# Deferring x0's scale and shift through DRAM, and moving GpSimd steps to VectorE, in a two-block transformer kernel

## The chip, the core and the metric

The kernel runs on one core of one Trainium2 chip. The metric is the device time of one execution in microseconds (us): the median of several runs, smaller is better. The core's compute engines are TensorE (PE in the profile; PEld is its weight load), VectorE (DVE), ScalarE (ACT) and GpSimd (POOL). SyncE (SP) issues the transfers between the chip's memory (DRAM) and the on-chip buffer. Each engine works through its own instructions in program order and waits for others by semaphores.

## The reference, cut to what matters

The sequence has T = 1024 rows of width D = 1024, in fp32. Two transformer blocks stand behind each other; the change touches the first up to the end of its mixer:

```python
x = layer_norm(x, ln0_g, ln0_b)                       # "x0"
mod = silu(c) @ w_ada + b_ada
sh_a, sc_a, gt_a, sh_f, sc_f, gt_f = split(mod, 6)    # 1024 columns each
h = x * (1.0 + sc_a) + sh_a
y = hybrid_mixer(h, w_in, ...)                        # gated delta rule (4 heads) and gated linear attention
x = layer_norm(ALPHA * x + (1.0 + gt_a) * y, ln1_g, ln1_b)
...                                                   # conv FFN, third norm, second block
```

In the mixer, `h @ w_in` gives q, k, v (through a short causal convolution and silu), gates and the inputs of the linear attention (GLA). The delta rule needs its decay gates (`log_a`, `beta`) before any head can start.

## The kernel before

Every large product runs as three fp32r products on PE (`mm3`, line 415): an operand is split into a high part (a cast on ACT, line 430) and a low part (a subtraction, line 433, on DVE unless a caller names POOL). PE transposes through line 419.

The order of the instructions is not written by hand. Parts of the work are Python generators, "streams", which a small planner (`Order`) interleaves: a stream yields a time or a condition, the planner's clock advances with each matmul that is emitted, and the stream due first goes on. When a stream is written with other yields, or emits other instructions, the rows of each engine interleave in another way. On-chip memory is handed out in pages (`Arena`): 128x1024 "full" or 128x512 "half"; the names pa, pg, y, wh, wl, wf in the rows are pages, opl and oph the low and high part of a left operand, b a PSUM bank.

What the change touches, in the order of time:

- `startup` normalizes x, makes the columns `sh_a`, `sc_a` from w_ada with multiply-adds on DVE (lines 765 and 767), and makes the first operand block by block: transposes on PE, then two ACT copies (lines 790, 791) and the subtraction for the low part (line 792, POOL). `w_take("A0")` splits the first weights.
- `x0_out` scales and shifts the normalized rows: for each of eight pages one DVE multiply (line 857) and one POOL add (line 858), then a store to `x0_d`. These rows are read back much later, behind the mixer.
- `delta_gates` (lines 1172 to 1212) makes the gates with some fifteen tiny DVE operations on 128x32 tiles (`dg_...`); the last one writes `dg_la` (line 1182), which PE needs for cumulative sums (`b<-dg_la,triu`), and with them the first head can start. The convolutions of q, k, v stand on the same engine: multiply-adds from PSUM (line 574), finished by line 1021.
- `mod_rest` makes the other four parts of `mod`, in eight chunks of 512 columns: eight loads of w_ada (256 KB each, two ahead) per chunk, each scaled on ACT (line 881) and added up on POOL (line 883; the first is copied, line 885).
- In the delta rule each unit of half a head has three POOL products of 128x512 (lines 1475, 1487, 1488), GLA one per head (line 1291). The gated output (`gate_op`) splits into high and low parts, with every second low part on POOL.

Of the kernel before, what the change touches and what calls it, by code (L numbers as in the profile page):

```python
# [169 lines left out]
def p3(ap, b=P):  # L170
    return ap.rearrange("p (a b) -> p a b", b=b)
# [139 lines left out]
class Kern:  # L311
# [398 lines left out]
    def startup(self):  # L710
# [38 lines left out]
        for h in range(2):  # L749
            for _ in self.ln_rows([p.ap for p in x[4 * h:4 * h + 4]]):  # L750
                pass
        wa = self.w_take("A0")
        hs, hb, tb = self.sm(), self.sm(), self.sm()
# [18 lines left out]
        def feed(k, acc):  # L772

            pm = self.ps()
            for c in (1, 0):
                for i in range(2):
                    self.mm(pm[:, c:c + 1], acc[:, i, c], self.ones[:, 0:1], i == 0, i == 1)

            c1 = slice(k, k + 1)
            V.scalar_tensor_tensor(hs[:, c1], pm[:, 1:2], b1[:, c1], self.ln0_g[:, c1], op0=OP.add, op1=OP.mult)  # L780
            V.scalar_tensor_tensor(tb[:, c1], pm[:, 1:2], b1[:, c1], self.ln0_b[:, c1], op0=OP.add, op1=OP.mult)
            V.scalar_tensor_tensor(hb[:, c1], pm[:, 0:1], self.b_ada[:, c1], tb[:, c1], op0=OP.add, op1=OP.add)
            self.psg(pm)
            for hf in range(2):
                h, l = self.op[hf]
                ps = self.ps()
                for t in range(4):
                    self.tr(ps[:, t * P:(t + 1) * P], x[4 * hf + t].ap[:, k * P:(k + 1) * P])
                f = fl[hf].ap
                S.activation(h[:, k], ps, AF.Identity, scale=hs[:, c1], bias=hb[:, c1])  # L790
                S.activation(f, ps, AF.Identity, scale=hs[:, c1], bias=hb[:, c1])
                G.tensor_tensor(out=l[:, k], in0=f, in1=h[:, k].bitcast(F32), op=OP.subtract)  # L792
                self.psg(ps)
# [9 lines left out]
        for j, ks in enumerate(blocks):  # L803
            acc = products(j)
            ada_load(1)
            for i, k in enumerate(ks):
                feed(k, acc[:, :, :, i * P:(i + 1) * P])
                if k:
                    use(k - 1)
# [14 lines left out]
    def start_rest(self):  # L824
        G = self.nc.gpsimd
        self.fb()
        G.tensor_scalar(self.hgain[:, 0:1], self.dnng, 0.5, None, op0=OP.mult)
        G.tensor_scalar(self.hgain[:, 1:2], self.glng, 0.5, None, op0=OP.mult)
        yield from self.x0_out(self.x)
        yield from self.mod_rest(self.cond)  # L830

# [7 lines left out]
    def x0_out(self, x):  # L839

        nc, I, A = self.nc, self.I, self.A
        self.x0_d = self.dram.tile([T, D], F32, name="x0_d")
        gr, br = self.gb
        for r, n in ((gr, "ln0_g"), (br, "ln0_b")):
            self.row_of(r.ap, I[n])
        yield 2.31
        nc.vector.tensor_scalar(br.ap, br.ap, ALPHA, None, op0=OP.mult)

        def out(t):
            nc.sync.dma_start(self.x0_d[t * P:(t + 1) * P, :], x[t].ap)  # L850
            A.give(x[t])
            self.x0_out_done.add(t)
            return
            yield
        for t in range(8):
            p = x[t].ap
            nc.vector.scalar_tensor_tensor(p, p, ALPHA, gr.ap, op0=OP.mult, op1=OP.mult)
            nc.gpsimd.tensor_tensor(p, p, br.ap, OP.add)
            self.o.spawn(out(t), 8)
            yield 3.92  # L860
        A.give(gr, br)

    def mod_rest(self, cond):
# [5 lines left out]
        for c in range(4, 12):  # L869
# [6 lines left out]
            for k in range(KT):  # L876
# [3 lines left out]
                a = wh[k % 3].ap  # L880
                nc.scalar.activation(a, a, AF.Copy, scale=cond[:, k:k + 1])
                if k:
                    nc.gpsimd.tensor_tensor(acc, acc, a, OP.add)  # L883
                else:
                    nc.gpsimd.tensor_copy(acc, a)
            A.give(*wh[1:])
# [377 lines left out]
    def gla_unit(self, p, hf, gls, q, k, gvp, att, St):  # L1264
# [25 lines left out]
        V.scalar_tensor_tensor(qd, q[:, hs], 0.125, t, op0=OP.mult, op1=OP.mult)  # L1290
        G.tensor_tensor(kn, k[:, hs], kdt, OP.mult)
        V.tensor_tensor(ke, ke, k[:, hs], OP.mult)
# [132 lines left out]
    def delta(self, h, kq, vp):  # L1425
# [10 lines left out]
        for hf in range(2):  # L1436
# [37 lines left out]
            V.scalar_tensor_tensor(Mn, Mn, 0.0, mb(self.mL), op0=OP.max, op1=OP.add)  # L1474
            G.tensor_tensor(qd, qd, p3(q_[:, c0 * P:(c0 + 4) * P]), OP.mult)
            S.activation(u["at"].ap, u["at"].ap, AF.Exp)
# [9 lines left out]
            V.tensor_scalar(nbr2, br2, -1.0, None, op0=OP.mult)  # L1486
            G.tensor_tensor(xk, kd, bc(xkc), OP.mult)
            G.tensor_tensor(kd, kd, bc(self.ekd[:, hc]), OP.mult)
            V.tensor_tensor(Mn, Mn, bc(nbr2), OP.mult)
# [206 lines left out]
    def gate_op(self, hf, k, z, done):  # L1696
# [7 lines left out]
        self.psg(ps)  # L1704
        self.split(z, h[:, k], l[:, k], lo_eng=G if k % 2 else V)
        self.A.give(*done)
# [96 lines left out]
    def x_ops(self, ready, free, evs, kept=None):  # L1803
# [5 lines left out]
        add, sub = OP.add, OP.subtract  # L1809
        yield ready  # L1810
        t3, t4, pages = [], [], []
        for j in range(4):
# [265 lines left out]
    def ffn(self, sc):  # L2078
# [70 lines left out]
        yield self.h2[0]  # L2149
        self.o.spawn(self.x_ops(self.h2[1], two, tev, self.xf))  # L2150
        self.o.spawn(self.res_rows(tev[1]))
# [1046 lines left out]
```

## Time and profile before

| | before |
|---|---|
| median of three runs | 2696.44 us (2691.53 to 2700.05) |
| profiled execution, its time | 2694.74 us |
| its span (first to last instruction) | 2693.0 us |
| mean granted TensorE clock | 0.989 |
| busy: PE, DVE, ACT, POOL | 95%, 73%, 49%, 15% |

The profiled execution is the one whose rows are read below; its own time stands 1.7 us over its span and 1.7 us under the median of the runs. A busy share is an average over the whole span. POOL has most of its work in the first quarter; DVE's share differs from stretch to stretch.

### The profile page before, as it was taken

Reading aid. Unit: us, or ns where it says so; the run is one execution under the profiler, and the core shown is the slowest. Engines: PE = TensorE matmul, PEld = TensorE weight load, DVE = VectorE, ACT = ScalarE, POOL = GpSimd, SP = SyncE. Lnnn points to the kernel's source line nnn. Section 1 sums busy time; section 2 is a strip of 40 time slices with the busy share of each in tenths; the row PEclk is TensorE's granted clock in tenths of the full one; section 3 lists DMA queues with packets and bytes.
Section 4 is the critical chain, followed back from the end, with each engine's and each line's share of the span. In section 5 each row is a group of like instructions: output and inputs, shape, how many; then the busy total and the mean of one; then the engine's idle time right before and its main releaser. Section 6 shows DMA issues by size and latency. Waiting matters only on the chain.

```text
span 2693.0 us, 35990 instructions
## 1 busy us (share of the span) xinstructions
PE 2569.3 (95%) x13053; PEld 2094.2 (78%) x13053; DVE 1954.4 (73%) x3264; ACT 1317.6 (49%) x2261; POOL 413.4 (15%) x472
## 2 busy tenths in 40 slices
PE   6889999999999999999989999999999999999998
PEld 4677888789877777788867666679878888888886
DVE  7875565457798897798976876775546866788774
ACT  4434544344544444464357867774444433344443
POOL 4633333332000000000140232310000000000002
PEclk9999999999999999999999999999999999999999
DMA  7423323565433433365311312166204345484541
GB/s 229 158 58 97 86 75 93 160 217 175 132 117 129 156 118 103 140 216 155 110 55 43 82 50 62 49 201 195 77 32 141 137 126 167 178 295 131 171 125 63
DMA packets 293218, 343.95 MB, mean 128 GB/s; under 512 B 32401, under 2 KB 217513, under 8 KB 293041
## 3 DMA queue, kind: packets, MB, share of 16 engines
q1 hardware_dynamic: 292656, 341.51, 39.9%
q8 instruction: 103, 1.69, 0.3%
q14 instruction: 74, 0.61, 0.1%
q10 hardware_dynamic: 385, 0.15, 0.0%
HBM read 244.12 MB, written 93.28 MB: 125 GB/s over the span
## 4 chain that ended last, share of the span: by engine, by line
PE 70%; DVE 13%; ACT 5%; POOL 4%; DMA 3%; issue 3%; SPq 0%; POOLq 0%; DVEq 0%; ACTq 0%
PE b L415 67%; PE b L419 3%; DVE wl L433 2%; POOL smalls L597 1%; DVE pg L2118 1%; DVE y L2118 1%; ACT wh L430 0%; POOL y L883 0%; DVE y L574 0%; DMA pa<-in_w_ada_dram 0%; DVE wf L2118 0%; DMA wf<-in_w_o_dram 0%; DMA pg<-in_w_ada_dram 0%; POOL rsv L596 0%; DVE y L2057 0%
## 5 line engine op out<-in xcount | busy, mean ns | idle before, releaser
L415 PE MATMUL b<-oph,wl 128*128 128x512 f32 (+1 forms) x1552 | 623.2, 403 | 12.2 <-ACT oph L670 8.6
L415 PE MATMUL b<-opl,wh 128*128 128x512 f32 (+1 forms) x1552 | 612.9, 395 | 0.6 <-POOL opl L792 0.6
L415 PE MATMUL b<-oph,wh 128*128 128x512 f32 (+1 forms) x1552 | 609.8, 393 | 0.0
L415 PEld LDWEIGHTS b<-oph,wl 128*128 128x128 f32 x1552 | 293.6, 189 | 77.4 <-ACT oph L670 8.8
L415 PEld LDWEIGHTS b<-opl,wh 128*128 128x128 f32 x1552 | 293.4, 189 | 62.3 <-issue 3.1
L415 PEld LDWEIGHTS b<-oph,wh 128*128 128x128 f32 x1552 | 293.0, 189 | 62.8 <-issue 1.5
L415 PE MATMUL b<-opl,oph 128*128 128x512 f32 x672 | 261.4, 389 | 0.0
L415 PE MATMUL b<-oph 128*128 128x512 f32 x672 | 261.4, 389 | 0.0
L415 PE MATMUL b<-oph,opl 128*128 128x512 f32 x672 | 261.3, 389 | 0.0
L430 ACT CAST oph<-pg 128x512 fp32r<-128x512 f32 (+1 forms) x202 | 125.4, 629 | 233.2 <-PE b L415 203.8
L415 PE MATMUL b<-wh,opl 128*128 128x256 f32 (+1 forms) x608 | 198.0, 326 | 0.9 <-DVE opl L433 0.7
L415 PE MATMUL b<-wl,oph 128*128 128x256 f32 (+1 forms) x608 | 193.5, 318 | 0.0
L415 PE MATMUL b<-wh,oph 128*128 128x256 f32 (+1 forms) x608 | 193.3, 318 | 0.0
L433 DVE TENSOR_TENSOR opl<-pg,oph 128x512 fp32r<-128x512 f32 (+1 forms) x210 | 144.1, 695 | 64.0 <-ACT oph L430 62.4
L433 DVE TENSOR_TENSOR wl<-wf,wh 128x1024 fp32r<-128x1024 f32 (+2 forms) x98 | 132.8, 1355 | 63.6 <-ACT wh L430 63.4
L430 ACT CAST wh<-y 128x512 fp32r<-128x512 f32 x164 | 101.9, 622 | 127.5 <-PE b L415 108.9
L430 ACT CAST wh<-wf 128x1024 fp32r<-128x1024 f32 (+2 forms) x98 | 112.4, 1147 | 79.9 <-PE b L415 46.0
L433 DVE TENSOR_TENSOR wl<-y,wh 128x512 fp32r<-128x512 f32 x164 | 112.7, 691 | 49.3 <-ACT wh L430 48.9
L415 PEld LDWEIGHTS b<-oph 128*128 128x128 f32 x672 | 126.1, 188 | 26.4
L415 PEld LDWEIGHTS b<-oph,opl 128*128 128x128 f32 x672 | 126.1, 188 | 26.4 <-ACT y L1993 0.2
L415 PEld LDWEIGHTS b<-opl,oph 128*128 128x128 f32 x672 | 126.1, 188 | 26.0
L415 PEld LDWEIGHTS b<-wh,opl 128*128 128x128 f32 x608 | 116.4, 192 | 11.1 <-issue 2.2
(1117 smaller groups left out, 5145.4 us busy)
## 6 DMA issues: line engine op xcount, KB each, us to landing
pg<-s_d SPq DMA_DIRECT2D x168, 256.0 KB
wf<-in_w_in_dram SPq DMA_DIRECT2D x48, 512.0 KB
y<-in_ffn_w_up_dram SPq DMA_DIRECT2D x31, 512.0 KB
s_d<-pg SPq DMA_DIRECT2D x31, 512.0 KB
s_d<-y SPq DMA_DIRECT2D x20, 512.0 KB
y<-in_w_mlp_in_dram SPq DMA_DIRECT2D x20, 512.0 KB
pa<-in_w_ada_dram SPq DMA_DIRECT2D x39, 256.0 KB
dn<-in_w_mlp_out_dram SPq DMA_DIRECT2D x18, 512.0 KB
```

The costliest lines, as they stand in the source:

```text
L415: self.nc.tensor.matmul(o, a, b, start=start, stop=stop, **kw)
L419: self.nc.tensor.transpose(o, a, self.ident if ident is None else ident)
L430: nc.scalar.copy(hi, src)
L433: (lo_eng or nc.vector).tensor_tensor(out=lo, in0=src, in1=hi.bitcast(F32), op=OP.subtract)
L597: nc.gpsimd.tensor_tensor(out, v[:, :n], self.mhalf[:, :n], OP.pow)
L2118: V.scalar_tensor_tensor(t[:, d:], x[:, :T - d], tap(2 - d, m), t[:, d:], op0=OP.mult, op1=OP.add)
```

## The change

The scale and shift of x0 no longer stand in `x0_out`: the normalized pages are stored to a scratch tensor in DRAM (`xh_d`) and given back at once. A new stream, `x0_rows`, starts 110 us of planner time later and does the work in 16 pieces of 128x512: load from `xh_d`, DVE multiply, DVE add, store to `x0_d`. In `mod_rest`, the ACT scaling and POOL addition of each piece become one DVE multiply-add. The low parts of the first operand, three products per delta rule unit, one product per GLA head, and the remaining low parts of `gate_op` move from POOL to DVE. `w_take("A0")` stands after the first block of the operand. Another edit, in `x_ops`, only makes an argument lazy.

```diff
164.09 1.11 PE L419 MATMUL b<-ident,pa 128*128 128x128 f32 x4 [6.10 <-DVE pa L1021] startup
-        wa = self.w_take("A0")
+        wa = []
...
-                G.tensor_tensor(out=l[:, k], in0=f, in1=h[:, k].bitcast(F32), op=OP.subtract)
+                V.tensor_tensor(out=l[:, k], in0=f, in1=h[:, k].bitcast(F32), op=OP.subtract)
...
                 feed(k, acc[:, :, :, i * P:(i + 1) * P])
+                if not k:
+                    wa += self.w_take("A0")
...
         yield from self.x0_out(self.x)
+        yield 25
         yield from self.mod_rest(self.cond)
164.09 1.11 PE L419 MATMUL b<-ident,pa 128*128 128x128 f32 x4 [6.10 <-DVE pa L1021] x0_out
-            nc.vector.scalar_tensor_tensor(p, p, ALPHA, gr.ap, op0=OP.mult, op1=OP.mult)
-            nc.gpsimd.tensor_tensor(p, p, br.ap, OP.add)
-            self.o.spawn(out(t), 8)
-            yield 3.92
-        A.give(gr, br)
+            self.nc.sync.dma_start(self.xh_d[t * P:(t + 1) * P, :], x[t].ap)
+            self.A.give(x[t])
+        self.A.give(*self.gb)
+        self.o.spawn(self.x0_rows())
...
+    def x0_rows(self):
+        nc, A, V = self.nc, self.A, self.nc.vector
+        yield 110
+        for c in range(2):
+            cs = slice(c * 512, (c + 1) * 512)
+            yield self.need(0, 3)
+            gb = A.half(), A.half()
+            for r, n in zip(gb, ("ln0_g", "ln0_b")):
+                self.row_of(r.ap, self.I[n][cs])
+            yield 5
+            for r in gb:
+                V.tensor_scalar(r.ap, r.ap, ALPHA, None, op0=OP.mult)
+            for t in range(8):
+                yield self.need(0, 1)
+                pg = A.half()
+                rows = slice(t * P, (t + 1) * P)
+                nc.sync.dma_start(pg.ap, self.xh_d[rows, cs])
+                yield 6
+                V.tensor_tensor(pg.ap, pg.ap, gb[0].ap, OP.mult)
+                V.tensor_tensor(pg.ap, pg.ap, gb[1].ap, OP.add)
+                nc.sync.dma_start(self.x0_d[rows, cs], pg.ap)
+                A.give(pg)
+                yield 8
+                if c:
+                    self.x0_out_done.add(t)
+            A.give(*gb)
164.09 1.11 PE L419 MATMUL b<-ident,pa 128*128 128x128 f32 x4 [6.10 <-DVE pa L1021] mod_rest
-                nc.scalar.activation(a, a, AF.Copy, scale=cond[:, k:k + 1])
                 if k:
-                    nc.gpsimd.tensor_tensor(acc, acc, a, OP.add)
+                    V.scalar_tensor_tensor(acc, a, cond[:, k:k + 1], acc, op0=OP.mult, op1=OP.add)
                 else:
-                    nc.gpsimd.tensor_copy(acc, a)
+                    V.tensor_scalar(acc, a, cond[:, 0:1], None, op0=OP.mult)
164.09 1.11 PE L419 MATMUL b<-ident,pa 128*128 128x128 f32 x4 [6.10 <-DVE pa L1021] GLA, delta rule, gate_op
-        G.tensor_tensor(kn, k[:, hs], kdt, OP.mult)
+        V.tensor_tensor(kn, k[:, hs], kdt, OP.mult)
...
-            G.tensor_tensor(qd, qd, p3(q_[:, c0 * P:(c0 + 4) * P]), OP.mult)
+            V.tensor_tensor(qd, qd, p3(q_[:, c0 * P:(c0 + 4) * P]), OP.mult)
...
-            G.tensor_tensor(xk, kd, bc(xkc), OP.mult)
-            G.tensor_tensor(kd, kd, bc(self.ekd[:, hc]), OP.mult)
+            V.tensor_tensor(xk, kd, bc(xkc), OP.mult)
+            V.tensor_tensor(kd, kd, bc(self.ekd[:, hc]), OP.mult)
...
-        self.split(z, h[:, k], l[:, k], lo_eng=G if k % 2 else V)
+        self.split(z, h[:, k], l[:, k])
```

How instructions move shows at three places. First VectorE, where the decay gates are made, before:

```order
L1021 SCALAR_TENSOR_TENSOR pa_103<-pa_101,pa_103 128x1024
...
L433 TENSOR_TENSOR wl_74<-wf,wh_73 128x1024
L1175 TENSOR_TENSOR dg_x<-dg_x,rb 128x32
...
L857 SCALAR_TENSOR_TENSOR y<-y,pa_98 128x1024
L1202 TENSOR_SCALAR dg_u<-dg_e 128x32
L857 SCALAR_TENSOR_TENSOR y<-y,pa_98 128x1024
L574 SCALAR_TENSOR_TENSOR pg<-b_77,hcv,pg 128x511
L1204 TENSOR_SCALAR dg_u<-dg_u 128x32
L857 SCALAR_TENSOR_TENSOR y<-y,pa_98 128x1024
...
L1212 SCALAR_TENSOR_TENSOR dg_x<-dg_x,dg_l 128x32
L1452 TENSOR_REDUCE smalls<-pa_106 128x4
L1182 SCALAR_TENSOR_TENSOR dg_la<-dg_x,dg_ea 128x32
```

And the same place in the changed program, whose lines stand 17 or 18 further down (its lines 900 and 902 are the multiply-add and the first product of `mod_rest`):

```order
L433 TENSOR_TENSOR wl_74<-wf,wh_73 128x1024
L1038 SCALAR_TENSOR_TENSOR pa_103<-pa_101,pa_103 128x1024
...
L574 SCALAR_TENSOR_TENSOR pg<-b_77,hcv,pg 128x511
L1227 TENSOR_TENSOR dg_l<-dg_l,dg_e 128x32
L902 TENSOR_SCALAR wh_630<-wh_630,cond 128x512
L574 SCALAR_TENSOR_TENSOR pg<-b_77,hcv,pg 128x510
L1228 TENSOR_TENSOR dg_l<-dg_l,dg_u 128x32
L900 SCALAR_TENSOR_TENSOR wh_630<-wl_631,cond,wh_630 128x512
L574 SCALAR_TENSOR_TENSOR pg<-b_77,hcv,pg 128x509
L1229 SCALAR_TENSOR_TENSOR dg_x<-dg_x,dg_l 128x32
L900 SCALAR_TENSOR_TENSOR wh_630<-wl_631,cond,wh_630 128x512
L1199 SCALAR_TENSOR_TENSOR dg_la<-dg_x,dg_ea 128x32
```

The 128x1024 multiplies of `x0_out` are gone from between the gate operations; three operations of `mod_rest` on freshly loaded pieces of w_ada stand there instead, and the subtraction for the weights has moved ahead of the second convolution's end (line 1021, now 1038). Second, PE at the gates: the block of matmuls into bank b_75 (q, k, v and z projections), before:

```order
L419 MATMUL b_80<-ident,pa_104 128x128 x4
L415 MATMUL b_75<-oph_66,wl_74 128x512
...
L415 MATMUL b_75<-opl_67,wh_73 128x512
L415 MATMUL b_75<-oph_66,wh_73 128x512
L415 MATMUL b_81<-dg_la,triu 128x32
L415 MATMUL b_81<-dg_la,ones 128x32
```

And in the changed program:

```order
L419 MATMUL b_80<-ident,pa_104 128x128 x4
L415 MATMUL b_75<-oph_66,wl_74 128x512
L415 MATMUL b_81<-dg_la,triu 128x32
L415 MATMUL b_81<-dg_la,ones 128x32
L415 MATMUL b_75<-opl_67,wh_73 128x512
L415 MATMUL b_75<-oph_66,wh_73 128x512
```

Before, nine matmuls of that block (the first two and last two rows stand around the mark) come ahead of the gate products, now one does: PE asks for `dg_la` eight matmuls earlier. Third, the queue of SyncE ahead of the gates in the changed program (wf is the next block of w_in, wh_630 and wl_631 the first pieces of w_ada for `mod_rest`):

```order
L846 DMA xh_d<-y 128x1024 x3
L463 DMA wf<-in_w_in_dram 128x8x128
L846 DMA xh_d<-y 128x1024 x3
L463 DMA wf<-in_w_in_dram 128x8x128
L846 DMA xh_d<-pg 128x1024 x2
L1434 DMA t_d_704<-y 128x344 x3
...
L463 DMA wf<-in_w_in_dram 128x8x128
L891 DMA wh_630<-in_w_ada_dram 128x512
L891 DMA wl_631<-in_w_ada_dram 128x512 x2
```

The loads for `mod_rest` stand right behind a load of wf, and a load of wf waits until DVE has read the wf before it (line 433). Before, the eight stores of x0 stood among and behind these loads, each waiting for POOL's add; now they stand ahead and wait for no engine's arithmetic on x0.

## Rows read from the trace of the kernel before

**Rows 1.** The page: busy per engine; share by engine of the chain; one group.

```profile
PE 2569.3 (95%) x13053; PEld 2094.2 (78%) x13053; DVE 1954.4 (73%) x3264; ACT 1317.6 (49%) x2261; POOL 413.4 (15%) x472
...
PE 70%; DVE 13%; ACT 5%; POOL 4%; DMA 3%; issue 3%; SPq 0%; POOLq 0%; DVEq 0%; ACTq 0%
...
L433 DVE TENSOR_TENSOR opl<-pg,oph 128x512 fp32r<-128x512 f32 (+1 forms) x210 | 144.1, 695 | 64.0 <-ACT oph L430 62.4
```

**Rows 2.** Waits of PE, 70 to 690 us: total us, times, longest us.

```profile
PE b L415 <- DVE dg_la L1182: 9.2, 1, 9.2
PE b L419 <- DVE pa L1021: 6.1, 1, 6.1
PE b L415 <- DVE y L1552: 3.9, 2, 2.7
...
PE b L419 <- DVE pg L1703: 0.2, 1, 0.2
```

**Rows 3.** Timeline of PE at the two large waits: start us, us, [idle before].

```profile
108.02 0.64 PE L415 MATMUL b<-dg_la,triu 128*128 128x32 f32 x2 [9.23 <-DVE dg_la L1182]
...
109.46 0.63 PE L415 MATMUL b<-opl,wh 128*128 128x512 f32 x1
109.89 0.63 PE L415 MATMUL b<-oph,wh 128*128 128x512 f32 x1
...
112.84 0.40 PE L415 MATMUL b<-oph,wh 128*128 128x512 f32 x1
113.08 0.40 PE L415 MATMUL b<-oph,wl 128*128 128x512 f32 x1
...
164.09 1.11 PE L419 MATMUL b<-ident,pa 128*128 128x128 f32 x4 [6.10 <-DVE pa L1021]
```

**Rows 4.** Timeline of DVE around the gates, 84 to 114 us.

```profile
84.95 2.68 DVE L1021 SCALAR_TENSOR_TENSOR pa<-pa,pa 128x1024 f32<-128x1024 f32 x1
...
88.88 1.21 DVE L433 TENSOR_TENSOR wl<-wf,wh 128x1024 fp32r<-128x1024 f32 x1
90.01 2.40 DVE L1175 TENSOR_TENSOR dg_x<-dg_x,rb 128x32 f32<-128x32 f32 x1
...
106.23 1.73 DVE L1182 SCALAR_TENSOR_TENSOR dg_la<-dg_x,dg_ea 128x32 f32<-128x32 f32 x1
...
110.70 0.18 DVE L1191 TENSOR_TENSOR dg_u<-b,Gc 128x32 f32<-128x32 f32 x1
...
113.96 0.74 DVE L574 SCALAR_TENSOR_TENSOR pg<-b,hcv,pg 128x509 f32<-128x509 f32 x1
```

**Rows 5.** Timeline of POOL in the same stretch.

```profile
88.92 3.44 POOL L858 TENSOR_TENSOR y<-y,pa 128x1024 f32<-128x1024 f32 x1
```

**Rows 6.** Groups of instructions, 0 to 70 us, DVE, then POOL.

```profile
L767 DVE SCALAR_TENSOR_TENSOR pa<-pa,cond,pa 128x512 f32<-128x512 f32 x6 | 8.1, 1421 | 0.0
L767 DVE SCALAR_TENSOR_TENSOR y<-pa,cond,y 128x512 f32<-128x512 f32 x6 | 6.1, 1083 | 0.0
...
L792 POOL TENSOR_TENSOR opl<-pa,oph 128x512 fp32r<-128x512 f32 x15 | 23.3, 1573 | 15.9 <-ACT pa L791 15.8
```

**Rows 7.** Busy time by stretch: length, then each engine's.

```profile
70.00:110.00 40.00, 30.77 (x139) 21.11 (x138) 38.25 (x54) 15.19 (x25) 21.62 (x11) 0.91 0.51 172
...
300.00:690.00 390.00, 377.23 (x2431) 329.29 (x2430) 231.24 (x409) 169.67 (x286) 119.22 (x139) 0.99 0.44 139
```

**Rows 8.** ACT's scaling in mod_rest (L881): idle before it until, us, times.

```profile
  DMA pg<-in_w_ada_dram: 26.4, 13
  DMA pa<-in_w_ada_dram: 18.9, 14
...
  DMA y<-in_w_ada_dram: 8.7, 3
```

**Rows 9.** One piece of w_ada: SP issues it.

```profile
213.86 0.35 SPq L873 DMA_DIRECT2D pa<-in_w_ada_dram  x1
```

**Rows 10.** The same piece: ACT has it.

```profile
216.95 0.72 ACT L881 ACTIVATE pa<-pa,cond 128x512 f32<-128x512 f32 x1 [1.35 <-DMA pa<-in_w_ada_dram]
```

More of the change, by code (lines that the diff above doesn't have):

```diff
@@ L839, in x0_out @@
     def x0_out(self, x):
-        nc, I, A = self.nc, self.I, self.A
         self.x0_d = self.dram.tile([T, D], F32, name="x0_d")
[L843 to L854, printed above, removed]
-        for t in range(8):
-            p = x[t].ap
-            nc.vector.scalar_tensor_tensor(p, p, ALPHA, gr.ap, op0=OP.mult, op1=OP.mult)
-            nc.gpsimd.tensor_tensor(p, p, br.ap, OP.add)
-            self.o.spawn(out(t), 8)
-            yield 3.92
-        A.give(gr, br)
+        for t in range(8):
+            self.nc.sync.dma_start(self.xh_d[t * P:(t + 1) * P, :], x[t].ap)
+            self.A.give(x[t])
+        self.A.give(*self.gb)
+        self.o.spawn(self.x0_rows())
+        return
+        yield
+    def x0_rows(self):
[24 more added lines that the diff above has]
+            A.give(*gb)
     def mod_rest(self, cond):
@@ L1810, in x_ops @@
         yield ready
+        kept = kept and kept()
         t3, t4, pages = [], [], []
@@ L2149, in ffn @@
         yield self.h2[0]
-        self.o.spawn(self.x_ops(self.h2[1], two, tev, self.xf))
+        self.o.spawn(self.x_ops(self.h2[1], two, tev, lambda: self.xf))
         self.o.spawn(self.res_rows(tev[1]))
```

## The prediction

> **What bounds the kernel now.** I read the page first: PE is busy 95% of the span, and the chain that ended last runs through PE for 70% of its length, through DVE for 13% and through POOL for 4% [rows 1]. So the time is PE's matmuls plus the gaps between them, and since the matmuls are not changed, an edit is worth what it does to PE's gaps. The second view is therefore the waits of PE over the stretch that the change touches. There the reader is to see two large ones and many small: 9.2 us for `dg_la`, 6.1 us for a convolution that line 1021 finishes (that of v for head 1), and 19 further groups from 3.9 down to 0.2 us, 20.7 us together [rows 2]. Nearly all are waits for DVE, whose work is late, not for POOL, whose work the change mostly moves.
>
> The third view is PE's timeline at the largest wait. PE stands from 98.79 to 108.02 for the gates, and afterwards its 512-column matmuls start 0.43 us apart (109.46, 109.89) before they are back at 0.24 (112.84, 113.08) [rows 3]. The first is the pitch of the lower clock level (1.2 GHz), the second that of the upper (2.4 GHz). From 108.02 to 112.84 PE worked at half speed, so the idle time costs another 2.4 us.
>
> The fourth view is DVE in the same stretch: it has hardly any idle time (38.25 of 40 us busy from 70 to 110 [rows 7]) and is late because of what stands between the gate operations. Six of the eight multiplies of x0 lie ahead of `dg_la`, each at least the 1.2 us of the like operation at 88.88; and tiny operations take far longer than they need. The addition of 128x32 at 90.01 took 2.40 us, the multiply-add that writes `dg_la` 1.73, where a like operation at 110.70 took 0.18 [rows 4]. At 90.01 POOL's add of x0, begun at 88.92, was running until 92.36 [rows 5], and the DVE addition ends 0.05 us behind it.
>
> **The change, part by part.** The total that moves to DVE: 16 low parts, 32 half-page operations for x0 instead of 8 multiplies of 1.2 us and one page of scaling, 64 multiply-adds, 28 products, 8 low parts of `gate_op`. By 0.695 us for a two-input operation of 128x512 [rows 1] and 0.74 for a multiply-add [rows 4] this is 11 + (22 + 2 - 10) + 47 + 19 + 6 = 97 us more on an engine that is busy 1954 us. Against it stand the collisions with POOL that go. What counts is where each lies.
>
> *The gates (term 1).* Ahead of `dg_la`, six multiplies (7 us) and the collisions (2.40 against 0.18, 1.73 against 0.18 and the like) go; one product and two multiply-adds of `mod_rest` come, at most 2.2 us. From the second convolution's end (begun at 84.95, 1.2 us without a collision) `dg_la` needs 2.5 us of tiny operations (some 14 at 0.18), three multiply-adds from PSUM (2.2) and those 2.2: ready at 93 if nothing else is waited for. But the first piece of w_ada is now in the way: its load stands behind a load of wf, which waits for the DVE subtraction that I read at 88.88, 1.21 us long [rows 4]; so it is issued at 87.5 (if that subtraction moves ahead of the second convolution, as the order shows) to 90.5. A piece landed 3.1 us after its issue (213.86 to 216.95) [rows 9, 10]. The product then starts at 91 to 94, and 2.5 to 3 us of DVE work stand between it and `dg_la`: ready at 94 to 97. PE asks for it eight matmuls of 0.24 us earlier than before, at 98.79 - 1.9 = 96.9. The gap is 0 to 1.5 us if these rows hold, and up to 4 if the stores of x0, 4 MB now issued at once, hold the pieces back. I take 1.0: 9.2 becomes 1.0, **-8.2 us**; with no gap of that length the slow clock behind it goes too, **-2.4** (bounds 0 and -2.4).
>
> *The convolution of v (term 2).* PE then arrives at the second wait about 10.6 us earlier, and DVE must have kept pace. Between `dg_la` and that convolution DVE loses two multiplies of x0 (2.4 us) and the collisions, and gets six or seven multiply-adds (5) and six products (4). PE's way from the gates to the wait is 50 us (108.02 to 157.99), DVE's was 56 (107.96 to 164.1) [rows 3, 4]. I put the gap at 5 instead of 6.1, **-1 us**, bounds -5 (no gap) and +5 (each multiply-add waits for its piece as ACT did).
>
> *Startup (term 3).* The 15 low parts in the stretch took 1.573 us each on POOL; DVE's multiply-adds beside them took 1.421 and 1.083 [rows 6] where 0.74 is the price without a collision [rows 4]: 12 x about 0.5 = 6 us lost in these two groups alone. Moving the work costs 16 x 0.695 = 11 us of DVE time and gives back 6 or more; PE's gaps in the stretch are small. I take **0**, bounds -4 and +5 (11 less 6). The Trainium skill, Perfetto Trace Analysis, section "Optimizing Scalar/DVE Operations", says that since the two engines share a read port, moving operations between them might not help; at startup the rows agree, and by that rule the sum would have 0 here as well.
>
> *The middle, 164 to 690 us (term 4).* From 300 to 690 DVE is busy 231 of 390 us [rows 7]; with all that could come there (97 less 11 at startup) it is at most 317, 81%. So throughput has room, but not order. ACT stood idle 26.4, 18.9 and 8.7 us, in 30 of its 64 scalings, until a piece had landed [rows 8], 1.8 us each time. These waits cost nothing on ACT; on DVE, which now takes the pieces itself, everything behind them waits: subtractions of weights, convolutions, norms, for which PE waits. The 16 pieces of x0 are loaded one step (6 us of planner time) ahead, where those of w_ada have two, so they will wait too. Against this, POOL's hops between DVE operations go, with their collisions. I take **+2**, bounds -10 (half of the 20.7 us of small waits) and +12.
>
> The sum: -8.2 - 2.4 - 1 + 0 + 2 = -9.6 us against the profiled execution's 2694.74 (1.7 under the median of the runs): 2685.1. Behind 690 us nothing is edited.
>
> **The rivals.** *VectorE's waits for transfers become PE's.* Place: the 390 us stretch, where DVE's slack is 390 - 317 = 73 us. For it: 54 us of waits move [rows 8], and 16 pieces of x0 with 1.8 us each add 29, together 83, more than the slack. Against it: a load issued earlier by an earlier DVE waits less, and PE's present waits there are short. If each of the 46 waits puts 0.45 us on PE, that is 21 us, in place of my +2: -9.6 + 19 = +9.4, 2704. It decides the sign from about 12 us on, and the verdict from 20.
>
> *Given back at the next wait.* Gates come earlier, but DVE does as much work as before between them and the convolution, and PE waits there 9 us longer instead: nearly nothing is left, -1 us, 2694. For it: after 108 DVE stays the later engine, and PE's largest wait behind the gates is for DVE [rows 2]. Against it: the collisions go. The rule of the Trainium skill named above would end here if it held at the gates too: as much DVE time comes as collisions go. There the rows disagree, since x0's multiplies leave DVE altogether.
>
> *More than that.* POOL's hops stood inside the small waits too, and half of the 20.7 us [rows 2] goes as well as 4 us at the convolution: -9.6 - 3 - 12 = -24.6, 2670. For it: collisions stretch DVE wherever POOL works (119 us of POOL from 300 to 690 [rows 7]). Against it: those waits are spread over 19 groups, and DVE gets more work there.
>
> **How the numbers follow.** About 8 us (0.3%) is what a measurement of this kernel can tell from no change. Chances: the forecast 0.52, with its own range of 2678 to 2692; DVE's waits 0.16; given back 0.18; more 0.14. Of the forecast 0.40 lies below 2688 and 0.12 above. Faster is 0.40 + 0.14 = 0.54; the same 0.12 + 0.15 (most of "given back") = 0.27; slower the rest, 0.19. The range takes in both outer rivals nearly whole and leaves out some 0.1 on each side: 2667 to 2706.
>
> **What would show it.** Right: PE's wait for `dg_la` (now line 1199) at 1.5 us or less, at about 97 us, and no 0.43 us pitch behind it; the tiny gate operations all under 0.4 us; a wait of 3 to 7 us for the convolution of v; L792's successor at 0.7 on DVE with multiply-adds of 0.74 beside it. Wrong: idle time of DVE ahead of the product of line 902 that ends with a landing of w_ada, above 3 us; PE's waits for DVE between 164 and 690 us that sum to over 30 us; or an earlier PE wait in startup, for a low part that stands behind DVE's multiply-adds. What would make the prediction wrong is above all the third kind of cost: waits of VectorE for pieces that were loaded late.

## The result, and the profile after

The changed kernel takes 2667.25 us (median of 4 runs, 2663.68 to 2673.79) against 2698.24 of the kernel before (4 runs, 2691.53 to 2701.88): a ratio of 0.989, 95% interval 0.9873 to 0.9907, or 25 to 34 us less. The forecast was 9.6 us less, with a range down to 2667: the direction was right, the size off by a factor of three, with the result at the very edge of the range.

In the diff of the change, the four lines that begin with 164.09 only name, by their last words, the function that the lines below them belong to; the row of PE in them is that of [rows 3] and no part of the change.

The profiled execution has a span of 2668.8 us, 24.2 less than before. The one before took 3.5 us less than the median of its kernel (2694.74 against 2698.24), the one after 3.3 us more (2670.58 against 2667.25), so the rows account for 24 of the 31 us. Its page, busy time of each engine:

```profile
PE 2569.5 (96%) x13053; PEld 2098.6 (79%) x13053; DVE 1986.2 (74%) x3407; ACT 1280.1 (48%) x2197; POOL 225.7 (8%) x348
```

PE is busy as long as before (2569.3) [rows 1], so the whole difference is in PE's gaps. DVE gained 32 us of busy time, not the 97 by which its work grew at unstretched prices: by an estimate from these two numbers, some 65 us by which POOL's work stretched DVE's before are gone. PE's waits from 70 to 690 us, in the columns of [rows 2]:

```profile
PE b L415 <- DMA y<-u_d: 7.8, 3, 4.4
PE b L419 <- DMA y<-mix_d: 5.1, 1, 5.1
PE b L415 <- DVE wl L900: 2.6, 1, 2.6
PE b L419 <- DVE y L1038: 1.9, 1, 1.9
```

Both large waits of [rows 2] are gone wholly: `dg_la` does not appear, and in the third of the stages below, where PE waited 6.1 us for the convolution of v for head 1, it waits for no convolution. The 1.9 us behind line 1038 (1021 before) lie in the fifth stage, at a later one. New are 12.9 us for two tensors that come back from DRAM: three waits for y from u_d (one of 0.2 us before) and one for y from mix_d (none before).

By stage, cut at the same places of PE's work (the gate products, the first transposes of `Gc` for the third unit, for the fifth, for the seventh, the first matmul of the out projection, the first of the FFN, and the first with the high and low part of one operand in it), before:

```profile
0.00:108.00 108.00, 73.15 (x343) 54.64 (x343) 86.50 (x156) 48.55 (x66) 51.25 (x55) 0.94 0.66 202
108.00:151.90 43.90, 43.88 (x219) 37.19 (x220) 38.63 (x63) 21.86 (x35) 29.25 (x20) 0.95 0.39 120
151.90:248.30 96.40, 85.96 (x588) 74.10 (x587) 65.29 (x171) 39.51 (x73) 29.39 (x26) 0.96 0.32 84
248.30:374.00 125.70, 119.09 (x708) 99.16 (x706) 79.83 (x162) 55.81 (x101) 36.36 (x37) 0.99 0.26 71
374.00:587.80 213.80, 205.87 (x1165) 170.51 (x1165) 106.20 (x195) 90.63 (x165) 77.29 (x102) 0.99 0.46 141
587.80:756.60 168.80, 162.36 (x1111) 148.51 (x1109) 133.98 (x233) 79.64 (x103) 25.07 (x23) 0.99 0.47 152
756.60:1150.80 394.20, 379.20 (x1633) 306.38 (x1634) 330.73 (x448) 189.62 (x281) 5.91 (x2) 1.00 0.41 136
```

And after (length, busy time of PE, PEld, DVE, ACT, POOL, then the granted clock):

```profile
0.00:90.10 90.10, 66.91 (x335) 50.21 (x336) 70.21 (x166) 45.76 (x62) 8.53 (x33) 1.00 0.82 256
90.10:133.60 43.50, 43.50 (x229) 36.70 (x229) 41.13 (x81) 19.86 (x31) 3.85 (x4) 1.00 0.28 75
133.60:233.10 99.50, 96.31 (x641) 83.03 (x639) 71.71 (x185) 35.44 (x65) 6.05 (x9) 1.00 0.35 96
233.10:361.30 128.20, 121.64 (x681) 102.94 (x680) 86.48 (x191) 48.85 (x90) 18.27 (x25) 0.89 0.36 104
361.30:574.90 213.60, 200.22 (x1118) 165.81 (x1117) 134.41 (x254) 70.12 (x131) 16.99 (x56) 0.96 0.52 162
574.90:736.90 162.00, 161.43 (x1133) 150.19 (x1132) 135.58 (x241) 75.35 (x95) 5.43 (x11) 1.00 0.46 152
736.90:1126.60 389.70, 378.94 (x1633) 305.96 (x1632) 333.85 (x453) 192.66 (x285) 5.95 (x2) 1.00 0.40 136
```

The matmuls of a stage (the count behind PE's time) are not quite the same before and after, because their order differs; so gaps compare better than lengths. Length less PE's busy time is PE's gaps. They change by -11.7 us up to the gates, 0, -7.2, 0, +5.5 in the last mixer stage, -5.9 in the out projection and -4.2 in the FFN's first half; 0.7 lie behind. The clock column tells the rest: 0.94 to 0.96 becomes 1.00 in the first three stages, but 0.99 becomes 0.89 in the fourth and 0.96 in the fifth.

Around the gates, the timeline of DVE after answers to [rows 4]:

```profile
80.31 1.22 DVE L1038 SCALAR_TENSOR_TENSOR pa<-pa,pa 128x1024 f32<-128x1024 f32 x1
...
81.66 0.19 DVE L1192 TENSOR_TENSOR dg_x<-dg_x,rb 128x32 f32<-128x32 f32 x1
...
85.91 0.49 DVE L902 TENSOR_SCALAR wh<-wh,cond 128x512 f32<-128x512 f32 x1
...
88.49 0.74 DVE L900 SCALAR_TENSOR_TENSOR wh<-wl,cond,wh 128x512 f32<-128x512 f32 x1
89.16 0.18 DVE L1199 SCALAR_TENSOR_TENSOR dg_la<-dg_x,dg_ea 128x32 f32<-128x32 f32 x1
```

The addition that took 2.40 us takes 0.19, and `dg_la` is there at 89.3. PE comes for it at 90.15 and goes on at the fast pitch (0.23 us from 90.82 to 91.05) [rows 3]:

```profile
90.15 0.30 PE L415 MATMUL b<-dg_la,triu 128*128 128x32 f32 x2
...
90.82 0.39 PE L415 MATMUL b<-oph,wh 128*128 128x512 f32 x1
91.05 0.40 PE L415 MATMUL b<-oph,wl 128*128 128x512 f32 x1
```

In startup, groups of the first 70 us as in [rows 6]:

```profile
L792 DVE TENSOR_TENSOR opl<-pa,oph 128x512 fp32r<-128x512 f32 x16 | 11.0, 686 | 1.9 <-ACT pa L791 1.9
...
L767 DVE SCALAR_TENSOR_TENSOR pa<-pa,cond,pa 128x512 f32<-128x512 f32 x6 | 4.4, 744 | 0.0
```

A low part takes 0.686 us where POOL took 1.573, and the multiply-adds beside it are at 0.74.

### The profile page after: what moved, and what is told of

It reads as the page before. It is cut to its first block, busy times and chain, and to the rows that moved or that the text cites. A ratio compares the mean times of both kernels' runs of the same rounds, so it can differ in the third digit from the quotient of the medians.

```text
span 2668.8 us, 35914 instructions
## 1 busy us (share of the span) xinstructions
PE 2569.5 (96%) x13053; PEld 2098.6 (79%) x13053; DVE 1986.2 (74%) x3407; ACT 1280.1 (48%) x2197; POOL 225.7 (8%) x348
## 5 line engine op out<-in xcount | busy, mean ns | idle before, releaser
L433 DVE TENSOR_TENSOR opl<-pg,oph 128x512 fp32r<-128x512 f32 (+1 forms) x218 | 149.9, 697 | 66.4 <-ACT oph L430 65.7
L433 DVE TENSOR_TENSOR wl<-wf,wh 128x1024 fp32r<-128x1024 f32 (+2 forms) x113 | 141.9, 1255 | 65.2 <-ACT wh L430 63.8
L430 ACT CAST wh<-wf 128x1024 fp32r<-128x1024 f32 (+2 forms) x113 | 121.7, 1077 | 82.5 <-PE b L415 59.1
L430 ACT CAST wh<-y 128x512 fp32r<-128x512 f32 x155 | 96.3, 623 | 111.7 <-PE b L415 97.0
L433 DVE TENSOR_TENSOR wl<-y,wh 128x512 fp32r<-128x512 f32 x155 | 105.3, 685 | 41.1 <-ACT wh L430 40.5
```

Source lines behind the costliest of these rows:

```text
L430: nc.scalar.copy(hi, src)
L433: (lo_eng or nc.vector).tensor_tensor(out=lo, in0=src, in1=hi.bitcast(F32), op=OP.subtract)
```

## The experiments

Names that begin with a_ take one part out of the changed kernel, with b_ put one part into the kernel before, with x_ vary the deferral, with m_ the modulation. Ratios are to the kernel before of the same batch of runs, with 95% intervals. Rows of the page and of waits are of each kernel's own profiled execution, one for each, so a few us between two of them can be chance. The `yield 25` ahead of `mod_rest` comes and goes with the deferral, except in x_hold and x_late. The later place of `w_take("A0")` is in the changed kernel and in all a_, x_ and m_ kernels, and in no b_ kernel: no run parts it from the rest.

Two theories stood at the start. Theory 1: each DVE operation beside a POOL one is stretched and, since DVE works in order, PE gets its input later, so each part gains in its own stage. Theory 2: only x0's multiplies in DVE's order mattered, the rest is an even trade. The others are put where the runs led to them.

**Taking one part out.**

a_low_pool:

```diff
-                V.tensor_tensor(out=l[:, k], in0=f, in1=h[:, k].bitcast(F32), op=OP.subtract)
+                G.tensor_tensor(out=l[:, k], in0=f, in1=h[:, k].bitcast(F32), op=OP.subtract)
```

> The changed kernel with the 16 low parts of the first operand back on GpSimd. Theory 1 (collisions: each VectorE operation that runs beside a GpSimd one is stretched, and since VectorE works in order, PE gets its input later; every part of the change then gains in its own stage): the multiply-adds of line 767 are back at 1.1 to 1.4 us instead of 0.74, small waits of PE and a stretch at the low clock return between 35 and 70 us, the gates come 5 to 7 us later, and the time is about 2673. Theory 2 (only the multiplies of x0 in VectorE's queue mattered, the rest is an even trade of GpSimd time for VectorE time): 2667 within 3.

Measured: 2678.75 us, ratio 0.9929 (0.9907 to 0.9952), some 11 us over the changed kernel (the intervals just touch). In the profiled executions, which lie 6.4 us apart, the stretch up to the gates is 2.7 us longer (92.8 against 90.1 us); the rest lies behind them. Not an even trade, but not all in its own stage either.

a_x0_inplace: `x0_out` of before, with its DVE multiplies and POOL adds, and no `x0_rows`.

```diff
         yield from self.x0_out(self.x)
-        yield 25
...
```

> The changed kernel with x0 scaled and shifted in place again (VectorE multiply, GpSimd add, store), everything else as changed. Theory 1: the wait of PE for the gates is back in part, 5 to 9 us with some 2 us of slow clock behind it, the rest of the gain stays: 2678 to 2682. Theory 2: nearly the whole gain is gone, 2690 or more.

Measured: 2672.36 us, 0.9904 (0.9884 to 0.9924). That interval overlaps the changed kernel's: the deferral, the first item of the change, is not shown to gain anything within it. Yet the wait for the gates is back and longer than ever (PE's timeline):

```profile
105.28 0.61 PE L415 MATMUL b<-dg_la,triu 128*128 128x32 f32 x2 [12.06 <-DVE pg L574]
```

The gate products come 15.1 us later than in the changed kernel (105.3 against 90.15), and the kernel makes it good behind them. Its fourth and fifth stage:

```profile
244.10:362.50 118.40, 114.73 (x697) 95.87 (x696) 81.97 (x178) 50.79 (x95) 16.11 (x21) 1.00 0.27 76
362.50:566.20 203.70, 201.43 (x1156) 167.18 (x1154) 123.47 (x235) 70.05 (x134) 19.50 (x58) 1.00 0.48 145
```

These take 322.1 us against 341.8, at clock 1.00 instead of 0.89 and 0.96, with 5.9 us of gaps instead of 19.9. Theories 1 and 2 both fall as they were put. At the first matmul of the out projection this kernel is 8.7 us ahead of the changed one (566.2 against 574.9 us). It loses that in the two stages behind the mixer:

```profile
566.20:733.10 166.90, 161.81 (x1119) 147.91 (x1116) 141.37 (x249) 76.34 (x97) 5.50 (x11) 1.00 0.49 157
733.10:1127.40 394.30, 379.60 (x1632) 306.43 (x1633) 330.29 (x448) 189.52 (x281) 5.77 (x2) 1.00 0.40 136
```

These are 9.5 us longer than the changed kernel's (162.0 and 389.7).

a_mod_act: `mod_rest` of before.

```diff
+                nc.scalar.activation(a, a, AF.Copy, scale=cond[:, k:k + 1])
                 if k:
-                    V.scalar_tensor_tensor(acc, a, cond[:, k:k + 1], acc, op0=OP.mult, op1=OP.add)
+                    nc.gpsimd.tensor_tensor(acc, acc, a, OP.add)
                 else:
-                    V.tensor_scalar(acc, a, cond[:, 0:1], None, op0=OP.mult)
+                    nc.gpsimd.tensor_copy(acc, a)
```

> The changed kernel with the multiply-adds of the remaining modulation back as ScalarE scaling and GpSimd adding. Theory 1: collisions are back from 95 to 560 us; the wait for the convolution of v (head 1) returns with 2 to 5 us and PE's small waits between 164 and 570 grow by some 5 us: 2673 to 2677. Theory 2: an even trade, 2667 within 3. A third theory, that VectorE's waits for the loaded pieces were a loss, would have it faster, 2660 to 2664.

Measured: 2700.89 us, 1.0026 (1.0008 to 1.0044): the whole gain is gone, 34 us, three to six times what theory 1 gave it. Its gates come at 90.5, as in the changed kernel; the next stage is 52.2 us long instead of 43.5, the fourth 132.3 instead of 128.2 and the fifth 226.1 instead of 213.6. Among PE's waits are:

```profile
PE b L415 <- POOL wl L901: 6.5, 1, 6.5
PE b L415 <- DVE pg L1511: 4.5, 1, 4.5
PE b L419 <- DVE pg L1039: 4.5, 1, 4.5
```

The last stands in the second stage, at 106.70, the two others in the fifth. The reason for the last stands in the timelines of POOL and DVE:

```profile
97.23 2.66 POOL L901 TENSOR_TENSOR wh<-wh,wl 128x512 f32<-128x512 f32 x2
99.98 0.26 POOL L596 TENSOR_SCALAR rsv<-smalls 128x8 f32<-128x8 f32 x1
100.32 1.67 POOL L597 TENSOR_TENSOR smalls<-rsv,mhalf 128x8 f32<-128x8 f32 x1
```

```profile
97.82 0.68 DVE L1486 TENSOR_TENSOR pa<-b,Gc 128x512 f32<-128x512 f32 x1
102.02 1.23 DVE L1500 TENSOR_SCALAR smalls<-smalls 128x4 f32<-128x4 f32 x1 [3.52 <-POOL smalls L597]
```

Each unit normalizes q and k with an inverse square root of 128x8 on POOL (lines 596, 597). Here it stands behind two additions of the modulation (97.23 to 99.9); DVE waits 3.5 us for it with everything that follows in its order, the convolution of line 1039 too, for which PE waits.

Ahead of the wait for line 1511, which ends at 431.99, the norm of a head's output goes the same way. It stands behind additions at 412.33 and 413.82, and DVE stands still for it:

```profile
417.20 2.29 DVE L1387 TENSOR_TENSOR pa<-pa,smalls 128x1024 f32<-128x1024 f32 x1 [3.80 <-POOL smalls L597]
```

Behind it DVE's operations beside further additions are stretched as well: line 1502 takes 1.18 us at 426.35, where it took 0.15 at 103.83. The 6.5 us are a third path: PE waits for the last sum of the modulation itself, on POOL; in the changed kernel it waits 2.6 us for that sum, on DVE. These are places, not the whole price: of the eight norms of q and k in this trace only the one at 99.98 starts right behind an addition.

a_prod_pool: the products of GLA and of the delta rule, and every second low part of `gate_op`, back on POOL.

```diff
-            V.tensor_tensor(xk, kd, bc(xkc), OP.mult)
+            G.tensor_tensor(xk, kd, bc(xkc), OP.mult)
...
-        self.split(z, h[:, k], l[:, k])
+        self.split(z, h[:, k], l[:, k], lo_eng=G if k % 2 else V)
```

> The changed kernel with the products of the delta rule and of GLA and every second low part of the gated output back on GpSimd. Theory 1: each product takes 1.3 to 1.8 us instead of 0.69 and stretches what runs beside it; the chain of each unit is longer by some 3 us, and PE's waits from 110 to 570 us grow by 3 to 8 us: 2670 to 2675. Theory 2: 2667 within 3.

Measured: 2678.0 us, 0.9926 (0.9902 to 0.9949), some 11 us over the changed kernel, with intervals that overlap by 0.0005. From the gates to the out projection PE has 8.3 us more gaps than in the changed kernel (31.5 against 23.1). Theory 1 fits in kind, at more than its number.

**Putting one part in.** The edits are those of the change, one at a time, without the later place of `w_take("A0")`.

> The kernel before with x0's scale and shift deferred alone. The runs so far let theory 1 and 2 both fall as they were put: taking the deferral out of the changed kernel cost 5 us only, though the wait for the gates came back with 12 us, and taking the modulation out cost everything. Theory 3: the deferral gains some 15 us up to the gates and gives about as much back between 230 and 580 us, where its transfers and its VectorE work make PE wait (for y from u_d and from mix_d). So here: the gates 10 to 15 us earlier, the stretch from the third to the last stage of the mixer 10 to 20 us longer, time 2692 to 2702. Theory 2 (the multiplies of x0 are the gain): 2675 or less.

b_x0: 2721.03 us, 1.0112 (1.0086 to 1.0139). The deferral alone loses 28 us, far more than theory 3 gave. The gates are early (94.3 us), but the four stages behind them take 526.4 us instead of 479.8, with PE waits like those of a_mod_act:

```profile
PE b L419 <- DMA y<-mix_d: 7.4, 1, 7.4
PE b L415 <- DMA y<-u_d: 6.9, 2, 6.1
PE b L415 <- POOL wl L899: 6.0, 1, 6.0
...
PE b L415 <- DVE pg L1509: 4.5, 1, 4.5
```

Behind the mixer the deferral gains: the out projection and the FFN's first half take 162.9 and 391.4 us here, 168.8 and 394.2 before.

> The kernel before with the remaining modulation alone on VectorE. Theory 3: the wait for the gates stays at 9 to 13 us or grows, the mixer behind it is 10 to 17 us shorter: 2680 to 2688. Theory 2: an even trade, 2697 within 3.

b_mod: 2680.26 us, 0.9954 (0.9939 to 0.9969): the only part that gains alone, 13 us, as theory 3 said; the gates' wait stays, at 9.0 us.

> The kernel before with the 16 low parts of the first operand alone on VectorE. Theory 1 and 3 alike: the stretch up to the gates 2 to 4 us shorter (multiply-adds back at 0.74 us), of which the gates' wait may take some back, since it hangs on VectorE: 2691 to 2696. Even trade: 2697 within 3.

b_low: 2691.51 us, 0.9992 (0.9983 to 1.0002), no difference that shows.

> The kernel before with the products of the delta rule, of GLA and the low parts of the gated output alone on VectorE. Theory 3: from the gates on 4 to 10 us shorter: 2687 to 2693. Even trade: 2697 within 3.

b_prod: 2696.63 us, 1.0009 (0.9994 to 1.0023), none either; theory 3's 4 to 10 us are refuted. So the four parts alone sum to about +17 us (27.9 - 12.9 - 1.7 + 3.4 against the median of their batch), and the whole change, which has the later `w_take` besides, gives -31: they work through each other.

> The kernel before with both the deferral and the modulation on VectorE, without the two other moves. Alone the first cost 28 us and the second gained 13. Theory 5 (the deferral brings the modulation's GpSimd additions next to the first units of the delta rule, where GpSimd's queue holds up their products and norms; on VectorE they don't): the two together gain, 2678 to 2688. If the parts simply add: 2708 within 4.

b_x0_mod, deferral and modulation together: 2690.38 us, 0.9981 (0.9961 to 1.0001). If the parts added, it would be about 2708; theory 5's 2678 to 2688 is missed by 2 us. Once x0 is deferred, the modulation on DVE is worth some 31 us instead of 13. The rest, some 23 us, comes with the other two moves and the later `w_take`, which b_x0_mod lacks too. Alone the two moves bring nothing; `w_take`'s place was not run alone.

**What the modulation on POOL costs.** Two variants of a_mod_act:

```diff
 m_noadd
-                if k:
-                    nc.gpsimd.tensor_tensor(acc, acc, a, OP.add)
-                else:
+                if not k:
                     nc.gpsimd.tensor_copy(acc, a)
 m_noscale
-                nc.scalar.activation(a, a, AF.Copy, scale=cond[:, k:k + 1])
```

> As a_mod_act (modulation back on ScalarE and GpSimd), but GpSimd's 56 additions are left out, ScalarE's scalings and all loads are kept (part of the computation is left out). Theory 6 (GpSimd's additions stand ahead of the small operations of the norms in GpSimd's queue, and VectorE and then PE wait for those; besides they stretch what runs beside them): nearly all of the 34 us comes back, 2667 to 2677. If ScalarE's scalings and its waits for the pieces are the cause: 2690 to 2701.

> As a_mod_act, but ScalarE's 64 scalings are left out and GpSimd adds the loaded pieces as they are, waiting for the loads itself (part of the computation is left out). Theory 6: 2690 to 2705, since the additions stay. If ScalarE is the cause: 2667 to 2677.

m_noadd: 2670.66 us, 0.9895 (0.9871 to 0.9919). m_noscale: 2707.7 us, 1.0039 (1.002 to 1.0058), 2.7 us over theory 6's range. Leaving out 56 additions on an engine that is 11% busy gives 30 us; leaving out ScalarE's 64 scalings gives nothing. So POOL's additions are the cost, as theory 6 has it. Without them PE hardly waits where it waited 4.5 us for line 1039 (now 1037):

```profile
102.54 0.66 PE L419 MATMUL b<-ident,pg 128*128 128x128 f32 x4 [0.77 <-DVE pg L1037]
```

How much of the 30 us is the queue (the norms behind the additions), how much the stretching beside them and how much the late last sum, these runs don't part. The queue is not shown to be most of it: from 60 to 690 us DVE's waits for line 597 sum to 27.6 us in a_mod_act, 22.0 in m_noadd and 19.5 in the changed kernel.

**What the deferred stream costs.** Theory 3 had its work or its transfers as the price.

```diff
 x_none     no x0_rows; x0_out stores to x0_d
 x_copy
-                V.tensor_tensor(pg.ap, pg.ap, gb[0].ap, OP.mult)
-                V.tensor_tensor(pg.ap, pg.ap, gb[1].ap, OP.add)
 x_nodma    as x_none, with the stream's VectorE operations on pages at hand
 x_actq
-                nc.sync.dma_start(pg.ap, self.xh_d[rows, cs])
+                nc.scalar.dma_start(pg.ap, self.xh_d[rows, cs])     # the store likewise
```

> The changed kernel without the deferred scale and shift: the normalized rows are stored raw straight to the tensor that is read back (part of the computation is left out). Theory 3 (the deferred stream costs some 20 us between 230 and 580 us): 2645 to 2650, and the waits for u_d and mix_d go. If the stream's work is hidden and the middle is longer for another reason: 2664 to 2668.

> The changed kernel whose deferred stream loads and stores its 16 pieces without the VectorE multiply and add (part of the computation is left out). Theory 3a (VectorE's 32 operations and its waits for the pieces are the cost): 2645 to 2652. Theory 3b (the transfers are the cost, by SP's order or by their volume): 2662 to 2668.

> The changed kernel whose deferred stream does the VectorE multiply and add on pages at hand, without loading or storing the 16 pieces (the rows are read back raw, part of the computation is left out). Theory 3a: 2660 to 2668. Theory 3b: 2645 to 2652.

> The changed kernel with the loads and stores of the deferred stream issued by ScalarE instead of SyncE, the computation whole. If SyncE's order is the cost (a store that waits for VectorE holds up the loads behind it): 2645 to 2655. If the transfers' volume, VectorE's work or the order of the program is the cost: 2664 to 2672, more where ScalarE is held up by the stores' waits.

Measured: x_none 2678.18 us, 0.9929 (0.9908 to 0.995); x_copy 2669.9, 0.9902 (0.9884 to 0.992); x_nodma 2669.94, 0.9898 (0.9875 to 0.992); x_actq 2675.33, 0.9924 (0.9909 to 0.994). None is faster than the changed kernel, and all lie 2 to 10 us over the higher of their two ranges. Neither the stream's DVE work nor its transfers nor SP's order is worth 20 us: theory 3 falls, in both forms. Up to the first matmul of the out projection x_none is 4.4 us ahead of the changed kernel (570.5 against 574.9 us); it loses 12.1 us in the two stages behind (168.7 and 395.1 us). What x_none, x_copy and x_nodma share with the changed kernel is a stretch of 27.3 us near 285 us at the low clock (from 283, 281 and 292 us); in x_actq it is 13.7 us. In the changed kernel:

```profile
240.00:288.00 48.00, 44.48 (x229) 35.17 (x227) 42.08 (x101) 22.58 (x36) 7.07 (x9) 1.00 0.57 164
288.00:315.30 27.30, 26.43 (x134) 24.68 (x135) 3.88 (x8) 4.72 (x11) 0.53 (x1) 0.50 0.14 38
```

From 288 to 315.3 PE is busy for 26.43 us and the clock is 0.50, 1.2 GHz; before it came a wait of 4.4 us for y from u_d. Two versions then moved the release of x0's pages:

```diff
 x_hold     raw stores at the old pace, no yield 25, x0_rows after 76 instead of 110
+        for t in range(8):
+            self.o.spawn(out(t), 8)
+            yield 3.92
 x_late     in place, 40 us later, one page per 6 us
+            V.tensor_tensor(p, p, gr.ap, OP.mult)
+            V.tensor_tensor(p, p, br.ap, OP.add)
```

> The changed kernel, whose raw stores of x0 (and so the giving back of its pages, the start of the remaining modulation and of the deferred stream) come at the pace of the kernel before, 3.92 us of planner time per page, instead of all at once. Theory 4 (not the deferred stream's work but the order that follows from pages and streams being free early costs: the projections' matmuls are used up by 280 us, PE then has some 30 us of small matmuls at the low clock): the stretch from 233 to 575 us is 10 to 20 us shorter, no low clock of 27 us near 285, gates as early as in the changed kernel: 2648 to 2658. Theory 4b (the gates being early is by itself what uses up the projections): the low stretch stays, 2662 to 2672.

> The changed kernel with x0 scaled and shifted in place, both operations on VectorE, one page each 6 us of planner time from 40 us later on, behind the gates: no trip through DRAM. Theory 4: pages come free later than in both kernels, the gates stay early (within 5 us of the changed kernel's), and if the middle keeps its projections: 2645 to 2660. Theory 4b: 2662 to 2672.

x_late: 2673.94 us, 0.9904 (0.9872 to 0.9937), 2 us over theory 4b's range, with a low stretch of that length too (from 245 us), which speaks for 4b. But a_prod_pool and b_x0_mod, whose gates are early as well (89.9 and 95.5 us), have only 6.8 and 10.2 us of low clock at that place (from 291 and 298 us), so early gates alone do not decide it. The price and the gain of the trip through DRAM are both within what these runs can tell. x_hold: 2684.55 us, 0.9948 (0.9923 to 0.9973), and its ten runs spread from 2673.74 to 2701.36; it lies over both ranges. Theory 4 falls: its profiled execution has three such stretches, of which one:

```profile
212.60:240.00 27.40, 27.40 (x142) 25.65 (x141) 4.92 (x13) 5.88 (x15) 0.00 (x0) 0.50 0.15 44
```

PE has no gap in it, it only runs at half speed.

## Why the prediction was wrong

By the prediction's own terms:

- **The gates (term 1), -10.6: right in mechanism and size.** The wait of 9.2 us is gone wholly, with the low clock behind it. `dg_la` was ready 0.8 us before PE came, both 5 to 8 us earlier than I had them, for startup is shorter too. I had `dg_la` up to 1.5 us late; my own times (ready by 97, asked for at 96.9) give only 0.1. The piece of w_ada in its way was no obstacle. But a_x0_inplace shows that these 11 us, which I took for most of the gain, are not needed for it.
- **The convolution of v (term 2), -1: mis-sized.** The wait of 6.1 us is gone, which is more than my bound of -5 for no gap at all, and the gaps of that stage fell by 7.2 us. I let DVE's new operations eat what it gained by the collisions. The norm that stands behind a modulation addition was in the trace of before already, and I gave it no price; there the timelines of POOL and of DVE read:

```profile
136.37 1.30 POOL L883 TENSOR_TENSOR y<-y 128x512 f32<-128x512 f32 x1
137.76 0.57 POOL L596 TENSOR_SCALAR rsv<-smalls 128x8 f32<-128x8 f32 x1
138.41 1.67 POOL L597 TENSOR_TENSOR smalls<-rsv,mhalf 128x8 f32<-128x8 f32 x1
...
140.12 0.17 DVE L1482 TENSOR_SCALAR smalls<-smalls 128x4 f32<-128x4 f32 x1 [1.89 <-POOL smalls L597]
```

  DVE stands still for 1.89 us in the very stretch in which it is late for this convolution.
- **Startup (term 3), 0: mis-sized.** Gaps up to the gates fell by 2.4 us besides the gates' own 9.2, and the clock no longer fell (0.94 became 1.00). I counted DVE's time for and against (11 and 6 us) and not what PE waited for: 2.0 us for the sums of line 767 and 0.6 us for the low parts in the first 70 us before, neither of them after. By the clock PE's work there is some 4 us shorter, an estimate: it is busy 6.2 us less with eight matmuls fewer, which are 1.9 us at 0.24. The rule of the Trainium skill that I weighed there (Perfetto Trace Analysis, section "Optimizing Scalar/DVE Operations": moving operations between the two engines might not help) agrees with b_low, which gains nothing alone, and not with a_low_pool, where the same move is worth some 11 us.
- **The middle (term 4), +2: right in sign, for another reason.** I feared 83 us of VectorE's waits for pieces. Line 900 waited 6.6 us for pieces in all, and lines 902 and 872 another 6.4 and 7.0:

```profile
  DMA pa<-in_w_ada_dram: 4.3, 6
  DMA y<-in_w_ada_dram: 2.1, 3
  DMA pg<-in_w_ada_dram: 0.2, 1
```

  One wait of 4.2 us ahead of line 902, the sign of being wrong that I named, did come; behind it stands the last sum, for which PE then waited 2.6 us. What the middle lost is 5.5 us of gaps in the fifth stage, where PE waited longest for y from mix_d (5.1 us) and from u_d (3.0 us), and the low clock near 288. Neither kind of wait is needed for the low clock: x_none, without the pieces of x0, and m_noadd, whose pieces of w_ada go to ACT, have the same stretch (from 283 and 285 us).
- **"Behind 690 us nothing is edited", 0: wrong.** The out projection and the FFN's first half have 10 us fewer gaps. No instruction there was edited; the order was: in all 19 kernels these two stages last either 162 to 165 and 388 to 392 us, or 166 to 169 and 393 to 398, and the first pair comes just with those whose page counts 113 casts of weights from the buffer wf, the second with those that count 98, 104 or 106. So the weights' preparation is ordered in another way, and the deferral brings that: a_x0_inplace, the changed kernel without it, counts 98 and takes 9.5 us longer there, and b_x0, the kernel before with it, counts 113 and takes 8.7 us less. The trip through DRAM is not what does it: x_late, which scales in place but later, counts 113 as well, and x_none and x_hold, which store the rows raw, count 104 and 106. Why this order is faster is open.

Two steps failed most. By stages it is the 0 behind 690 us, a term that I put at nothing because no line there was edited: 10.1 us of gaps went in the out projection and the FFN's first half. By parts it is the pricing of POOL: I priced its operations by what they cost DVE and hid the rest as "hops" within term 4, where I held the modulation's move to be a loss. Operations of 0.3 and 1.7 us on POOL stood behind modulation additions in some units, and such a wait passed through DVE's order to PE; m_noadd against a_mod_act puts 30 us on those additions, by this and the other paths together. Besides, I added terms. The parts don't add: the deferral brings the modulation forward, next to the first units, where it hurts on POOL (b_x0, +28) and not on DVE (b_x0_mod, 0.9981). That the direction came out is in part luck: the deferral, which I credited with most of the gain, loses 28 us alone, and the move that I held to be a loss is the only part that gains alone.

Open stay: why two moves that gain nothing alone (b_low, b_prod) are worth some 11 us each in the whole; what the later `w_take` is worth; what decides whether a low stretch of 27 us sets in after some wait; and how the deferral comes to change the order behind 575 us.

## What to carry to other kernels

An engine that is 11% busy can still cost 1% of the time: look at what stands in its queue ahead of the small operation that a busy engine waits for, at what runs beside it, and at the end of its chain, and try the kernel without that work. When a part of a change frees a stream to start earlier, ask what that stream puts beside its new neighbours, and try parts in pairs, since single ones told the wrong story here twice. Read gaps and granted clock by stage before crediting an edit: a wait of 12 us at the gates cost nothing that could be told in the end, and one program's time moved by 28 us while its granted clock went from 0.979 to 0.988. Look at stages without an edit too: 10 of the 24 us of gaps lay there.

## What the hardware showed that was not expected

A stretch at the low clock can last 27.3 us though PE is busy without a gap (27.40 of 27.40 us in x_hold), and whether it sets in differs from execution to execution of one program: the ten runs of x_hold have mean granted clocks from 0.979 (2701.36 and 2694.97 us) to 0.988 (2673.74), those of the changed kernel 0.985 (2673.79), 0.986 (2670.58) and 0.989 (2663.92 and 2663.68). At 13.6 us for each stretch of 27.3, an estimate for work that fills it at half speed, one or two stretches more or less would make most of the spread of both; only the profiled executions show the stretches themselves.
